# First mixer: the attention's calls placed between the k of the convolution's products

## The chip, the cores and the metric

The kernel runs on one core of one Trainium2 chip. The metric is the device time of one execution in microseconds (us). Three runs of the kernel before gave a median of 2560.59 us.

## What is computed

Two transformer blocks on 512 tokens of width 1024, all in float32. The change lies in the mixer of the first block. Cut to what matters there:

```python
px = modulate(rmsnorm(x, norm_mix), m3, m4) @ w_mix_in          # 512 tokens
pc = modulate(rmsnorm(ctx, norm_mix), mc3, mc4) @ w_mix_in      # 256 context tokens
q, k, v, gb, gc, u = split_heads(px, q_norm, k_norm)            # 8 query heads of 64, 2 key heads
qc, kc, vc, ... = split_heads(pc, q_norm, k_norm)
a  = softmax(rope(q) @ [kc, rope(k)].T / 8) @ [vc, v]           # 8 heads, 768 keys
sc = gb * short_conv3(gc * u, conv_w)                           # 512 channels
x  = x + m5 * (concat([rmsnorm(a), rmsnorm(sc)]) @ w_mix_out)
```

Products are done in three float32r passes (high times high, low times high, high times low), so that each k of a product is three matmuls per output piece.

## The kernel before

The program is traced with a framework that plans each engine's order: of the instructions that the plan takes as ready, the one that stands first in the program's text goes first. Text order is therefore a priority, and not yet the order on the engine. The semaphores come from the framework. `tc.issue_after(ins)` adds an edge of order between `ins` and the block's instructions on the same engine alone.

`run(jobs, bg)` (L180) goes through a list of jobs. A job loads its weights one job ahead, splits them (ACT makes `wh` at L159, DVE makes `wl` at L148), runs one `gemm` (L220) into one of two PSUM tiles `mm`, and evacuates the tile. After each job `bg(i)` is called. A `gemm` has a loop over k of `mm3` (L204): the three passes. After each k it counts `self.step` up and, if something is in `self.events`, calls `tick` (L211), which traces all due events inside `issue_after` of the last matmul. `later(steps, fn)` puts an event there. Other stages use it; the first mixer does not.

In `mixer1` (L623) the stages are:

- k, v and four q jobs. They use the PSUM pool `pm1`. After them `pm1` is closed and `pm2` opened in its place, with the one tile `sx` (tag `s2`, `ns2 = 1`) of the scores and two banks of tag `t`.
- The convolution: 12 jobs (`cc`, `cu`, `cb` for each of four j), each a `gemm` of 8 k over 256 and 258 columns. That is 96 k, and 24 x 2 matmuls a job.
- `r_from_acc(rc)` (L860), the norm of the convolution's output, and 8 output jobs on it (`job_out(co, f, False)`), each 4 k of 512 columns: 12 matmuls. Their evacuation (`tu`, then `x`) needs `rc`.
- `finish` (L864), which is put in as number 7 of that list, so before the eighth output job. It drains what is left of the attention and makes `ra`, the norm of the attention's output.
- 8 output jobs on the attention's output (`job_out(ao, f, True)`), whose evacuation needs `ra`.

The attention is a generator (L788). It keeps up to three units alive, of 16 in all (8 heads by two halves of the queries), and goes round them. A unit (L742) has four yields: two steps with scores (`sx` on PE, its maximum on DVE, `pp` = exp on ACT, reciprocal on DVE, scaling on ACT), one with 12 transposes and their splits (`pt`, `pth`, `ptl`), and one with 12 matmuls of probabilities by values (L776), `pv` and `at`. The fifth `next` on a unit finds its end, does no work, and the generator yields all the same (L794 to L797). So the whole attention takes 80 calls of `next(gen)`: 64 with work and 16 without. Call them n = 0 to 79. `bg` makes five of them after every job: n = 0 to 59 in the 12 jobs of the convolution, n = 60 to 79 after the first four output jobs.

The order of the calls that matter below: n = 44 and 46 are the score steps 18 and 19 (counted from 0), n = 59, 61, 62 the steps 24, 25, 26, n = 64, 65, 68, 74, 76 the steps 27 to 31, n = 63, 67, 71, 77 the transposes of units 12 to 15, n = 66, 70, 73, 78 their products by the values.

The attention's last product by the values feeds `make_y` and `sq_add` (L784, L785), these feed `ra`, and this the evacuation of the first two attention output jobs.

Of the kernel before, what the change touches and what calls it, by code (L numbers as in the profile page):

```python
# [120 lines left out]
class K:  # L121
# [501 lines left out]
    def mixer1(self, yc):  # L623
# [3 lines left out]
        with ExitStack() as es:  # L627
# [103 lines left out]
            jobs = [([(W[4], 1024)], job_k), ([(W[5], 1024)], job_v)]  # L731
# [56 lines left out]
            def attention():  # L788
                act = []
                todo = [(h, half) for h in range(8) for half in range(2)]  # L790
                while todo or act:
                    if todo and len(act) < 3:
                        act.append(unit(*todo.pop(0)))
                    for u in list(act):  # L794
                        if next(u, "end") == "end":
                            act.remove(u)
                        yield  # L797
            gen = attention()

            def bg(i):  # L800
                for _ in range(5):
                    next(gen, None)


            hold = {}
# [1 line left out]
            def job_in(nm, j):  # L807
                def go(ws):
                    t = p2.tile([P, 514], F32, name=nm, tag=nm, bufs=1) if nm != "cc" else pool.tile([P, 768], F32, name=nm, tag="to", bufs=2)
                    if nm == "cu":  # L810
                        u = pool.tile([P, 768], F32, name="cx", tag="to", bufs=2)[:, :512]
                        x_in(ws, u)
                        gcu = hold["cc"]
                        nc.vector.memset(t[:, 0:1], 0.0)
                        nc.vector.memset(t[:, 513:514], 0.0)
                        self.tt(t[:, 1:513], u, gcu[:, :512], ALU.mult)
                        w = lambda i: self.vec("conv_w", 4 * i + j)
                        self.ts(sct[j], t[:, 0:512], w(0), ALU.mult)
                        self.stt(sct[j], t[:, 1:513], w(1), sct[j], ALU.mult, ALU.add)
                        self.stt(sct[j], t[:, 2:514], w(2), sct[j], ALU.mult, ALU.add)  # L820
                    elif nm == "cc":
                        x_in(ws, t[:, :512])
                        hold["cc"] = t
                    else:
                        x_in(ws, t[:, :512])
                        self.tt(sct[j], sct[j], t[:, :512], ALU.mult)
                        self.sq_add(j, sct[j], 0, 512, p2)
                        self.dump("sc", j, sct[j])
                return go

            jobs = []
            for j in range(4):
                jobs += [([(W[10 + j], 1024)], job_in("cc", j)), ([(W[14 + j], 1024)], job_in("cu", j)),
                         ([(W[6 + j], 1024)], job_in("cb", j))]
            self.run(jobs, bg)

            g7 = pool.tile([P, 8], F32, name="g7")
            self.stt(g7, self.mx[:, 7, :], 1.0, self.vec("norm_ffn2", 0, 8), ALU.add, ALU.mult)

            def job_out(ops, f, last):  # L840
                def go(ws):
                    ps = self.mmtile()
                    self.gemm([ps[:, :512]], ws, 4, lambda k: [ops[k]])
                    t = pool.tile([P, 770], F32, name="tu", tag="tu", bufs=2)[:, :512]
                    self.tt(t, ps[:, :512], (ra if last else rc)[:, :512], ALU.mult)
                    self.stt(self.x[f], t, self.mx[:, 5, f:f + 1], self.x[f], ALU.mult, ALU.add)
                    if last:
                        self.dump("x2", f, self.x[f])
                        self.make_y(f, self.x[f], g7[:, f:f + 1], self.yh[f][:, :512], self.yl[f][:, :512])
                        for i in range(2):  # L850
                            self.split(self.yh[f][:, 512 + i:513 + i], self.yl[f][:, 512 + i:513 + i], self.mx[:, 6, f:f + 1])
                        self.sq_add(f, self.x[f], 0, 512, p2)
                return go
# [8 lines left out]
            ra = pool.tile([P, 770], F32, name="to", tag="to", bufs=2)  # L862

            def finish(ws):  # L864
                for _ in gen:
                    pass
                self.r_from_acc(ra, [(512, 0, 512)], pool, bank, n=512)

            jobs = [([(wo[f, :, 4:8, :], 512)], job_out(co, f, False)) for f in range(KD)]
            jobs.insert(7, ([], finish))  # L870
            jobs += [([(wo[f, :, 0:4, :], 512)], job_out(ao, f, True)) for f in range(KD)]
            self.run(jobs, bg)
            self.r_from_acc(self.r, [(0, 0, 256), (256, 256, 256)], pool, bank)


# [849 lines left out]
```

## Time and profile before

| | us |
|---|---|
| median of 3 runs | 2560.59 (2557.4 to 2562.12) |
| the profiled execution: time | 2563.32 |
| the profiled execution: span | 2561.5 |
| first mixer's convolution, attention and output: first to last score step begins | 679.5 to 822.1 |

The busy time of PE is a modelled one: matmuls are pipelined and their ends overlap, so gaps between starts say more than busy time. [...] Windows are in us from the span's start.

### The profile page before, as it was taken

How to read it: one execution, taken by the hardware profiler on the slowest of the kernel's cores; microseconds unless marked ns; L12 is line 12 of the kernel's file. 1: busy time of each engine (PE TensorE's matmuls, PEld its weight loads, DVE VectorE, ACT ScalarE, POOL GpSimd, SP SyncE). 2: the span in 40 equal slices, each digit the busy share in tenths (PEclk: the TensorE clock that was granted, in tenths of full speed). 3: DMA queues.
4: the chain of work that ended last, by engine and by line, in shares of the span. 5: the costliest groups of instructions: out<-in, count | busy, mean ns of one | idle time of the engine just before them, and what ended most of it. 6: DMA issues, size and time to landing. Idle time of an engine off the chain costs nothing.

```text
span 2561.5 us, 35787 instructions
## 1 busy us (share of the span) xinstructions
PE 2521.7 (98%) x13975; PEld 2171.1 (85%) x13975; DVE 1652.0 (64%) x3353; ACT 1115.9 (44%) x2052; POOL 15.6 (1%) x11
## 2 busy tenths in 40 slices
PE   7999999999999999999999999999999999999999
PEld 4889889899898888888888888888888877788887
DVE  7865664346888943335877776878888867633333
ACT  7221221234687532224677762655544444422221
POOL 2000000000000000000000000000000000000000
PEclk8999999999999999999999999999999999999999
DMA  7433543212111333333311122222222222233332
GB/s 265 143 113 107 177 145 122 66 51 81 60 38 38 100 99 99 91 103 95 101 58 58 58 84 83 73 63 80 61 74 77 75 89 88 92 94 98 96 101 84
DMA packets 85258, 235.71 MB, mean 92 GB/s; under 512 B 19840, under 2 KB 22592, under 8 KB 85088
## 3 DMA queue, kind: packets, MB, share of 16 engines
q1 hardware_dynamic: 85088, 233.42, 29.3%
q8 instruction: 110, 1.80, 0.3%
q14 instruction: 60, 0.49, 0.1%
HBM read 228.07 MB, written 5.31 MB: 91 GB/s over the span
## 4 chain that ended last, share of the span: by engine, by line
PE 91%; DVE 4%; ACT 3%; issue 1%; DMA 1%; DVEq 0%; ACTq 0%
PE mm L204 71%; PE mX L204 3%; PE mT L204 3%; PE pt L766 1%; PE pt L776 1%; PE e L1553 1%; DVE wl L148 1%; PE e L1563 1%; PE pv L1199 1%; PE sx L750 1%; PE e L1545 1%; PE e L1546 1%; PE z L204 1%; DMA araw<-wada 1%; PE e L1559 1%
## 5 line engine op out<-in xcount | busy, mean ns | idle before, releaser
L159 ACT ACTIVATE wh<-raw 128x1024 fp32r<-128x1024 f32 (+2 forms) x371 | 374.9, 1012 | 944.7 <-PE mm L204 567.1
L148 DVE TENSOR_TENSOR wl<-raw,wh 128x1024 fp32r<-128x1024 f32 (+2 forms) x371 | 431.1, 1163 | 165.6 <-ACT wh L159 160.6
L204 PE MATMUL mm<-yh,wh 128*128 128x512 f32 (+3 forms) x1552 | 455.9, 339 | 10.3 <-ACT yh L159 4.3
L204 PE MATMUL mm<-yl,wh 128*128 128x512 f32 (+3 forms) x1552 | 454.9, 338 | 0.0
L204 PE MATMUL mm<-yh,wl 128*128 128x512 f32 (+3 forms) x1552 | 451.5, 336 | 0.0
L204 PEld LDWEIGHTS mm<-yh,wh 128*128 128x128 f32 x1552 | 265.3, 189 | 44.9 <-issue 6.8
L204 PEld LDWEIGHTS mm<-yl,wh 128*128 128x128 f32 x1552 | 265.0, 189 | 29.9 <-issue 2.0
L204 PEld LDWEIGHTS mm<-yh,wl 128*128 128x128 f32 x1552 | 264.6, 189 | 29.2 <-issue 1.0
L204 PE MATMUL mm<-hl,wh 128*128 128x384 f32 (+1 forms) x704 | 227.4, 364 | 0.7 <-DVE hl L148 0.7
L204 PE MATMUL mm<-hh,wh 128*128 128x384 f32 (+1 forms) x704 | 227.3, 363 | 0.8 <-ACT hh L159 0.8
L204 PE MATMUL mm<-hh,wl 128*128 128x384 f32 (+1 forms) x704 | 227.8, 364 | 0.0
L204 PE MATMUL mm<-zh,wh 128*128 128x512 f32 x576 | 224.1, 389 | 0.0
L204 PE MATMUL mm<-zl,wh 128*128 128x512 f32 x576 | 224.1, 389 | 0.0
L204 PE MATMUL mm<-zh,wl 128*128 128x512 f32 x576 | 224.1, 389 | 0.0
L204 PEld LDWEIGHTS mm<-hh,wh 128*128 128x128 f32 x704 | 130.2, 189 | 15.0 <-ACT hh L159 1.1
L204 PEld LDWEIGHTS mm<-hl,wh 128*128 128x128 f32 x704 | 130.0, 188 | 14.8 <-DVE hl L148 1.0
L204 PEld LDWEIGHTS mm<-hh,wl 128*128 128x128 f32 x704 | 130.3, 189 | 13.8
L204 PEld LDWEIGHTS mm<-zh,wl 128*128 128x128 f32 x576 | 108.1, 188 | 22.6
L151 DVE SCALAR_TENSOR_TENSOR aacc<-araw,csil,aacc 128x1024 f32<-128x1024 f32 x70 | 88.3, 1282 | 60.4 <-DMA araw<-wada 60.3
L204 PEld LDWEIGHTS mm<-zl,wh 128*128 128x128 f32 x576 | 108.1, 188 | 22.4
L204 PEld LDWEIGHTS mm<-zh,wh 128*128 128x128 f32 x576 | 108.1, 188 | 22.3
L151 DVE SCALAR_TENSOR_TENSOR x<-mm,g,x 128x512 f32<-128x512 f32 x48 | 35.9, 747 | 115.3 <-PE mm L204 115.3
(504 smaller groups left out, 4550.0 us busy)
## 6 DMA issues: line engine op xcount, KB each, us to landing
raw<-win SPq DMA_DIRECT2D x88, 512.0 KB, 3.5
araw<-wada SPq DMA_DIRECT2D x60, 512.0 KB, 3.9
raw<-w1i SPq DMA_DIRECT2D x44, 512.0 KB, 3.7
raw<-w2i SPq DMA_DIRECT2D x44, 512.0 KB, 3.5
raw<-w3i SPq DMA_DIRECT2D x44, 512.0 KB, 3.5
raw<-wmi SPq DMA_DIRECT2D x18, 512.0 KB, 3.5
raw<-wbd SPq DMA_DIRECT2D x16, 512.0 KB, 3.7
raw<-w1o SPq DMA_DIRECT2D x16, 448.0 KB, 3.5
```

Of the source, the lines that this page charges most:

```text
L148: return self.V.tensor_tensor(out=out, in0=a, in1=b, op=op)
L151: return self.V.scalar_tensor_tensor(out=out, in0=a, scalar=s, in1=b, op0=op0, op1=op1)
L159: return self.A.activation(out=out, in_=a, func=func, bias=bias, scale=scale, **kw)
L204: last = self.T.matmul(o, lhsT=w[a], rhs=yy[b], start=start and i == 0, stop=stop and i == 2)
L750: self.T.matmul(sx[:, :512], lhsT=lq, rhs=kk[:, :512], start=i == 0, stop=i == 1)
L766: self.T.transpose(ps[:, (2 * kt + qt) * P:(2 * kt + qt + 1) * P], pr[qt][:, (2 * c + kt) * P:(2 * c + kt + 1) * P], self.cs("ident"))
L776: self.T.matmul(ps[:, :256], lhsT=vs[:, kt, g, :], rhs=pp[kt // 2][i][:, (kt % 2) * 256:(kt % 2 + 1) * 256], start=kt == 0 and i == 0, sto ...
L1199: self.T.matmul(pv[:, c0:], lhsT=a[:m, j], rhs=b, start=j == 4 and i == 0, stop=i == 2, skip_group_check=True)
L1545: self.T.matmul(ps[:, :256], lhsT=ch(kt, c), rhs=S0, start=True, stop=True)
L1546: self.T.matmul(ps[:, 256:], lhsT=ch(qt, c, 0), rhs=S0, start=True, stop=True)
L1553: self.T.matmul(ps[:, :256], lhsT=ch(XT, c, 0), rhs=vi, start=True, stop=True)
L1559: self.T.matmul(ps[:, 256:], lhsT=ch(kd, c, 0), rhs=vn, start=True, stop=True)
```

## The change

The five calls after each job are taken away. Before the convolution's jobs, 64 events are put on the step counter: call n is due after k number 3 + floor(3n/2) of what follows, counted over the `gemm`s. They are traced in `tick`, so each call's PE instructions get an edge of order behind the last matmul of that k, and in the text they stand there, ahead of the rest of the job. The 96 k of the convolution hold the calls n = 0 to 62; n = 63 is due at number 97, the first k of the first output job. Both `bg` are taken away, the one of the output jobs too. `finish` flushes the events and then drains the generator as before: n = 64 to 79 are traced there, after the text of seven output jobs.

```diff
-            def bg(i):
-                for _ in range(5):
-                    next(gen, None)
+
+            for n in range(64):
+                self.later(3 + 3 * n // 2, lambda: next(gen, None))
...
-            self.run(jobs, bg)
+            self.run(jobs)
...
             def finish(ws):
+                self.flush()
                 for _ in gen:
                     pass
                 self.r_from_acc(ra, [(512, 0, 512)], pool, bank, n=512)
...
-            self.run(jobs, bg)
+            self.run(jobs)
```

## Rows read from the trace of the kernel before

**Rows 1.** The page, parts 1 and 2.
```profile
span 2561.5 us, 35787 instructions
...
PE 2521.7 (98%) x13975; PEld 2171.1 (85%) x13975; DVE 1652.0 (64%) x3353; ACT 1115.9 (44%) x2052; POOL 15.6 (1%) x11
```

**Rows 2.** Windows of the stage; columns in the first row.
```profile
core 0: us, PE busy (x) PEld busy (x) DVE busy (x) ACT busy (x) POOL busy (x), PEclk, DMA share, GB/s
690.00:698.00 8.00, 5.48 (x35) 4.17 (x34) 6.70 (x15) 7.30 (x14) 0.00 (x0) 1.00 0.06 26
698.00:787.30 89.30, 89.18 (x691) 84.62 (x690) 73.98 (x153) 73.03 (x139) 0.00 (x0) 1.00 0.10 34
798.00:807.00 9.00, 6.94 (x30) 5.26 (x29) 8.86 (x21) 7.78 (x17) 0.00 (x0) 0.81 0.09 29
807.00:836.00 29.00, 29.00 (x173) 24.19 (x172) 24.10 (x47) 20.15 (x37) 0.00 (x0) 1.00 0.16 52
```

**Rows 3.** L750, the score steps: ns min/median/max, first and last start.
```profile
L750 PE MATMUL sx<-ksh,qs x32: 390/489/628, 679.5 to 822.1; 128*128 128x512 f32 x32
```

**Rows 4.** PE groups by form, first row 679.4 to 787.3, second 767.46 to 787.3.
```profile
L204 PE MATMUL mm<-yl,wh 128*128 128x258 f32 x76 | 21.9, 288 | 0.0
...
L204 PE MATMUL mm<-yl,wh 128*128 128x258 f32 x16 | 4.5, 282 | 0.0
```

**Rows 5.** Timeline of PE: score steps 18 and 19; columns in the first row.
```profile
start us, us, engine line op out<-in xcount [idle before <-releaser]
760.39 0.50 PE L750 MATMUL sx<-ksh,qs 128*128 128x512 f32 x1
761.19 0.28 PE L204 MATMUL mm<-yl,wh 128*128 128x256 f32 x1
767.45 0.40 PE L750 MATMUL sx<-ksh,qs 128*128 128x512 f32 x1
```

**Rows 6.** Timeline of ACT: the exp of score step 18 ends.
```profile
764.28 0.20 ACT L159 ACTIVATION_READ_ACCUMULATOR pp<-sx,st 128x1 f32 x1
```

**Rows 7.** Timeline of PE: first, last matmul of an output job, next job's first.
```profile
833.18 0.40 PE L204 MATMUL mm<-yh,wh 128*128 128x512 f32 x1
...
835.75 0.39 PE L204 MATMUL mm<-yh,wl 128*128 128x512 f32 x1
835.98 0.39 PE L204 MATMUL mm<-qs,wh 128*128 128x512 f32 x1
```

**Rows 8.** Timeline of PE: the wait for `rc`, and what follows it.
```profile
800.24 0.39 PE L204 MATMUL mm<-yh,wl 128*128 128x512 f32 x1
802.42 0.87 PE L766 MATMUL pt<-cst,pp 128*128 128x128 f32 x6 [1.80 <-ACT pp L159]
803.56 0.79 PE L204 MATMUL mm<-yh,wh 128*128 128x512 f32 x1 [0.26 <-DVE tu L148]
804.58 0.63 PE L750 MATMUL sx<-ksh,qs 128*128 128x512 f32 x1
805.86 0.63 PE L204 MATMUL mm<-yh,wl 128*128 128x512 f32 x1
```

**Rows 9.** Timeline of PE: the last two score steps.
```profile
818.72 0.50 PE L750 MATMUL sx<-ksh,qs 128*128 128x512 f32 x1
822.14 0.39 PE L750 MATMUL sx<-ksh,qs 128*128 128x512 f32 x1
```

**Rows 10.** Timeline: attention's last product, `ra` finished, third attention output job.
```profile
833.06 0.28 PE L776 MATMUL pt<-ptl,vs 128*128 128x256 f32 x1
842.06 0.69 DVE L151 SCALAR_TENSOR_TENSOR to<-rv,to 128x512 f32<-128x512 f32 x1
843.62 0.70 PE L204 MATMUL mm<-qs,wh 128*128 128x512 f32 x2 [0.82 <-DVE tu L148]
```

**Rows 11.** Windows around the wait for `rc` (columns as in Rows 2).
```profile
803.00:804.00 1.00, 0.74 (x4) 0.50 (x3) 1.00 (x2) 1.00 (x3) 0.00 (x0) 0.64 0.00 0
804.00:805.00 1.00, 1.00 (x3) 0.72 (x3) 1.00 (x4) 0.97 (x3) 0.00 (x0) 0.50 0.00 0
```

## Prediction

> **What bounds the kernel now.** I read the page first: PE is busy for 98% of the span [rows 1], so only what leaves PE without work, or lets it work slowly, can move the time much. Then I cut the first mixer into windows [rows 2]. From 698 to 787.3, the convolution with the attention between its products, PE has work for 89.18 of 89.30 us: no placing of the same work can gain there. Stalls stand at two places: 690 to 698 (5.48 busy of 8.00, 2.5 lost) and 798 to 807 (6.94 of 9.00, and a granted clock of 0.81). From 807 to 836 PE is busy for all 29.00 us again. So the most that better placing could win in this stage is those two places, some 5 to 6 us, 0.2%. What it can lose is open: it is the time that the attention takes by itself once nothing is left to lay beside it.
>
> The attention by itself is a chain. All 32 score steps share one PSUM tile, so a step starts when the exp of the step before has read it. They begin at 679.5 and the last begins at 822.1 [rows 3]: 142.6 us over 31 steps, 4.6 us each. The shortest distance that I found late in the stage is 3.42 us [rows 9], with output products in between.
>
> Where do they stand against their calls? Between 679.4 and 787.3 one of the six kinds of convolution matmul appears 76 times [rows 4], so some 20 of 96 k were done when the first score step began. By then the kernel before had made 10 calls and the new text would have made 12. The attention starts late and runs with a debt.
>
> Score step 18 begins at 760.39 and step 19 only at 767.45 [rows 5], though the exp that frees the tile ended at 764.48 [rows 6]. Sixteen of the 96 k remain at that moment [rows 4], so step 19 (n = 46) starts right after the tenth job, which is exactly where `bg` calls it. For 3 us PE had convolution products to run that stood earlier in the text, and ran them. That row is what I rest on: **a call that stands late in the text waits as long as PE has products that stand ahead of it.**
>
> **The change part by part.**
>
> Convolution, n = 0 to 62. The calls stand some five k earlier than before (n = 46 at k 72, not 80). The new edges of order bind on PE alone, behind a matmul that has long been issued, since the attention runs with a debt; so they add nothing. No semaphore is waited for anew. The calls issue no DMA, so nothing moves on SP's queue, and nothing of them is on POOL. On DVE and ACT they now stand ahead of the job's own evacuation; its cover is the second `mm` tile, which gives a job's length. Before, PE paid for such crowding 2.5 us at 690 to 698; I keep that, since calls 0 to 9 stand ahead of that evacuation in both texts. The gain is that steps 19 and on are no longer held: from 760.39 at 4.6 us a step, step 26 (n = 62) comes at 797.2, about 1.5 us earlier than now. PE has no idle time there to give back, so this gain is worth only what it takes off the end of the attention.
>
> Output jobs. Before, calls 60 to 79 stood after the first four output jobs. Now the text has seven output jobs, and only then n = 64 to 79: score steps 27 to 31, 36 transposes, four products by values. An output job is 12 matmuls from 833.18 to 835.98 [rows 7], 2.8 us. The work that stands ahead, counted from the convolution's end at 787.3: seven jobs, 19.6 us; steps 25 and 26 at 0.8 us each (760.39 to 761.19, [rows 5]), 1.6; two sets of transposes at about 1.1 (six in 0.87 with their end, [rows 8]), 2.2; a product by values, some 1.4 (an estimate from its 12 starts that end at 833.06, [rows 10]); the four matmuls for `rc`, about 1. Together 25.8 us, so PE comes free at 813.1, if it never waits for `rc`.
>
> Does it? Now the first evacuation with `rc` lets PE go on at 803.56 [rows 8]. If `rc` comes no sooner, the first two jobs and the rest are done at some 799.2, PE waits 4.4 us, step 27 slips into that hole, and the seventh job ends at 817.5. So either step 27 starts at 813.1 and four steps follow, or step 28 at 817.5 and three follow. At 3.42 us a step the last score step starts at 826.8 or 827.8, at 4.6 us at 831.5 or 831.3. The two ways agree: **826.8 to 831.5, where it now stands at 822.1**, 4.7 to 9.4 us later. I take the upper part, 8 us: 3.42 is the shortest distance that I found, and 4.6 the mean of all 31.
>
> What follows the last score step is a chain, 822.14 to 833.06 for the last product by values and 843.62 for the third attention output job, which waits for `ra` with 0.82 us of idle time [rows 9, 10]. Now the eighth output job and the first two attention jobs fill 8.4 us of it; after the change they have nothing to do with its length. Less crowding may take 1 us off, PE's pauses may add as much; both at nothing, bounds -1 and +2. The attention output jobs and all later stages are the same work and shift as a whole. Removing `bg` and adding `flush` costs nothing: all 64 events have fired when `finish` comes.
>
> The sum: the profiled execution took 2563.32 us, 2.73 above the median of the runs shown. It becomes 2571.3, and the median 2560.59 + 8 = **2568.6 us**.
>
> **The rivals.**
>
> *Not held.* If the plan finds moments when no output product is ready (a weight split late, a tile not evacuated), the steps 27 to 31 slip in, since each needs but 0.8 us of PE. Then only the gain counts: 13 steps after 760.39 at 4.6 us put the last step at 820.2, 1.9 us earlier, and with the pause before 803.56 and its slow matmuls avoided (about 2 us idle and 1.5 us slow) up to 5.4 us: 2555 to 2558.7. For it: the third and later jobs each wait for an evacuation. Against it: that evacuation is one DVE instruction of 0.7 us behind a job of 2.8 us, and [rows 5]. It decides if two or more of the five steps slip in.
>
> [...]
>
> *It does not do what it says.* The attention starts 20 k late and its pace is set by the one score tile, so "two for every three" never binds; if the plan also fills the output jobs as it does now, the order on PE hardly changes: -2 to +3 us, around 2561.
>
> **How the numbers follow.** Held as in the sum, +4 to +11 us: 0.50. Cold drain, +11 to +18: 0.12. Not held: 0.20. No effect: 0.18. The measurement can tell about 0.2%, 5.1 us, from no change. Slower by more than that: nearly all of the cold drain and 0.84 of the forecast, 0.54 together. Faster by more than that: a third of "not held", 0.07, and 0.01 for what I overlook. The same: 0.38. The range takes in "not held" at its best and all but the worst of the cold drain: 2555 to 2577.
>
> **What would show it.** Right: score steps close to 4.6 us apart up to the convolution's end; then a gap in them of 10 us or more while output jobs run without a pause; four or five score steps after the seventh output job with PE idle between them; the third attention output job near 851. Wrong: score steps among the third to seventh output jobs, or the last one before 823. [...] A new PE wait for `tg` or `tu` in the convolution would mean that crowding on DVE, which I put at nothing, is the cost.

## The result, and the profile after

The changed kernel takes 2572.41 us (median, 2572.2 to 2574.03), the kernel before 2560.28 us beside it: 12.1 us slower by the medians, which is 0.47%; the ratio on record is 1.0052 with a 95% interval of 1.0039 to 1.0066. Forecast were 2568.6 us and 2555 to 2577.

The profiled run of after, the slowest of its four, took 2574.03 us with a span of 2572.2 us. The page's part 1 looks like that of before [rows 1]:

```profile
span 2572.2 us, 35788 instructions
...
PE 2525.1 (98%) x13975; PEld 2172.9 (84%) x13975; DVE 1652.2 (64%) x3353; ACT 1119.2 (44%) x2052; POOL 15.5 (1%) x11
```

The same 13975 matmuls, and 98% again. The difference is in one stage. The first score step begins at 677.3 here and at 679.5 before [rows 3], so this run came 2.1 us earlier to the mixer (why, at the end). From that step to the end of the span it needs 2572.2 - 677.33 = 1894.87 us, before 2561.5 - 679.47 = 1882.03: **12.8 us are lost between, and all of them before 855**, since from there on the two traces run at one distance within 0.4 us. In the text below, "shifted" means 2.14 us added to a time of after, so that it can stand beside one of before.

The score steps of after, first as a group, then one by one from step 27 on, the second row being the first output product after `rc` (timeline of PE; "..." marks rows left out):

```profile
L750 PE MATMUL sx<-ksh,qs x32: 392/478/653, 677.3 to 830.8; 128*128 128x512 f32 x32
```

```profile
799.67 0.50 PE L750 MATMUL sx<-ksh,qs 128*128 128x512 f32 x1
...
804.56 0.50 PE L204 MATMUL mm<-yh,wh 128*128 128x512 f32 x1 [0.80 <-DVE tu L148]
...
818.59 0.39 PE L750 MATMUL sx<-ksh,qs 128*128 128x512 f32 x1
...
823.38 0.46 PE L750 MATMUL sx<-ksh,qs 128*128 128x512 f32 x1
...
826.88 0.51 PE L750 MATMUL sx<-ksh,qs 128*128 128x512 f32 x1
...
830.81 0.50 PE L750 MATMUL sx<-ksh,qs 128*128 128x512 f32 x1
```

Step 27 comes at 799.67, while PE waits for `rc`. Then none comes for 18.92 us, although the exp that frees the score tile for step 28 ended at 809.08 (timeline of ACT):

```profile
808.89 0.19 ACT L159 ACTIVATION_READ_ACCUMULATOR pp<-sx,st 128x1 f32 x1
```

For 9.5 us its tile was free and step 28 did not run. Windows show what PE does in that time, and what follows (columns as in Rows 2; PEclk is the granted clock of PE as a share of the full one):

```profile
698.00:787.30 89.30, 89.28 (x694) 84.92 (x693) 73.61 (x153) 73.72 (x134) 0.00 (x0) 1.00 0.11 34
...
804.50:818.50 14.00, 13.94 (x60) 11.34 (x61) 11.07 (x23) 4.36 (x7) 0.00 (x0) 1.00 0.33 97
...
834.00:854.00 20.00, 12.78 (x39) 8.94 (x40) 9.54 (x17) 7.88 (x13) 0.00 (x0) 0.66 0.04 14
```

In the gap PE runs 60 output products, five jobs of twelve, without a pause. Behind the last score step it has work for 12.78 of 20 us, and the granted clock is 0.66 in the mean. Before, the stretch around and behind the last score step was full: PE busy for 29.00 of 29 us up to 836, at 1.00 [rows 2]. What PE waits for there are the links of one chain: exp, transposes, split, product by values, evacuation, `make_y`, sum of squares (two matmuls at L275, below called the sums of `ra`), `ra`. In the timeline of PE it looks like this:

```profile
834.71 0.33 PE L766 MATMUL pt<-cst,pp 128*128 128x128 f32 x1 [1.39 <-DVE at L148]
837.44 1.54 PE L766 MATMUL pt<-cst,pp 128*128 128x128 f32 x6 [2.40 <-ACT pp L159]
839.75 1.11 PE L766 MATMUL pt<-cst,pp 128*128 128x128 f32 x4 [0.77 <-DVE ptl L148]
...
845.01 0.51 PE L204 MATMUL mm<-qs,wh 128*128 128x512 f32 x1 [1.68 <-ACT qs L159]
...
846.49 2.04 PE L275 MATMUL t<-acc,cst 128*128 128x512 f32 x2
849.90 1.22 PE L204 MATMUL mm<-qs,wh 128*128 128x512 f32 x2 [1.38 <-DVE tu L148]
...
854.34 0.63 PE L204 MATMUL mm<-qs,wh 128*128 128x512 f32 x2
```

The wait at 849.90 is not one for `ra`, which is finished on DVE only at 852.69 (last row here). It is one for the evacuation of the eighth output job, which DVE makes at 849.17, right behind the first instruction of the norm for `ra`:

```profile
848.56 0.69 DVE L156 TENSOR_SCALAR rv<-t 128x512 f32<-128x512 f32 x1 [0.88 <-PE t L275]
849.17 0.68 DVE L148 TENSOR_TENSOR tu<-mm,to 128x512 f32<-128x512 f32 x1
...
852.00 0.69 DVE L151 SCALAR_TENSOR_TENSOR to<-rv,to 128x512 f32<-128x512 f32 x1
```

The 12.8 us add up along that chain. From the first to the last score step: 153.48 us, before 142.67 [rows 3, 9], **10.81 more**. From the last score step to the end of `ra`: 852.69 - 830.81 = 21.88 us, before 842.75 - 822.14 = 20.61 [rows 9, 10], **1.27 more**. The remaining 0.8 us lie behind `ra`: the third attention output job began 0.87 us after the end of `ra` before (843.62) and begins 1.65 us after it now (854.34), since from 849.90 on a pair of output products takes 1.22 us, at a granted clock of 0.50, where it takes 0.63 at 854.34, at 1.00.

### The profile page after: what moved, and what is told of

Its sections match the earlier page's. It is cut to its first block, busy times and chain, and to the rows that moved or that the text cites. A ratio compares the mean times of both kernels' runs of the same rounds, so it can differ in the third digit from the quotient of the medians.

```text
span 2572.2 us, 35788 instructions
## 1 busy us (share of the span) xinstructions
PE 2525.1 (98%) x13975; PEld 2172.9 (84%) x13975; DVE 1652.2 (64%) x3353; ACT 1119.2 (44%) x2052; POOL 15.5 (1%) x11
## 4 chain that ended last, share of the span: by engine, by line
PE 91%; DVE 4%; ACT 3%; issue 1%; DMA 1%; SPq 0%; DVEq 0%; ACTq 0%
PE mm L204 71%; PE mX L204 3%; PE mT L204 3%; DVE wl L148 1%; PE pt L776 1%; PE pt L766 1%; PE e L1554 1%; PE sx L750 1%; PE e L1564 1%; PE pv L1200 1%; PE e L1546 1%; PE e L1547 1%; PE z L204 1%; PE e L1560 1%; DMA araw<-wada 0%
```

## The experiments

One measure is used for all kernels. In windows of 2 us from 670 to 880, "without work" is the sum of 2 minus PE's busy time, and "slow" the sum of PE's busy time times (1 minus granted clock): an estimate of what the same work would have saved at the full clock, from pairs like the one above (1.22 us at 0.50, 0.63 at 1.00). The ratio of each kernel is to runs of the kernel before on the same chip (their median is 2560.3 us for after and e1 to e4, 2561.0 for the others).

| kernel | median us | ratio to before, 95% | without work | slow | both |
|---|---|---|---|---|---|
| before | 2560.3 | | 7.1 | 1.6 | 8.6 |
| after | 2572.4 | 1.0039 to 1.0066 | 12.4 | 6.6 | 19.0 |
| e1, five per output job | 2558.85 | 0.9986 to 1.0004 | 6.0 | 0.0 | 6.0 |
| e2, removed only | 2580.47 | 1.0067 to 1.0095 | 17.2 | 8.5 | 25.7 |
| e3, eighty placed | 2561.01 | 0.9996 to 1.0014 | 7.6 | 0.0 | 7.6 |
| e4, third | 2572.83 | 1.0038 to 1.0063 | 13.1 | 5.1 | 18.2 |
| e5, third, own scratch | 2561.86 | 0.9996 to 1.0014 | 8.3 | 0.0 | 8.3 |
| e6, first, own scratch | 2558.48 | 0.9981 to 0.9998 | 5.7 | 0.0 | 5.7 |
| e7, filler | 2571.83 | 1.0028 to 1.0053 | 5.1 | 0.0 | 5.1 |
| e8, first, shared | 2578.22 | 1.0051 to 1.0079 | 16.4 | 4.7 | 21.0 |
| e9, changed, own scratch | 2574.23 | 1.0038 to 1.0066 | 14.4 | 6.5 | 21.0 |
| e10, before, own scratch | 2560.47 | 0.9987 to 1.0005 | 6.4 | 3.3 | 9.7 |

Sums may be off by 0.1 from rounding. Apart from e7, which has 50 matmuls more, the kernels fall into two groups in the last column as they do in the first: up to 9.7 us in those near 2560, 18 and more in those above 2572. The measure isn't exact and does not order the kernels within a group: after has 10.4 more than before and lost 12.8, e8 has 12.4 more and lost 17.3 by the medians. What makes up the rest is open. Of the 6.6 of after, 1.5 lie at 690 to 698, at the start of the convolution, and have nothing to do with its end.

**e1: the calls given back to the output jobs** (the last `run` is that of the output jobs).

```diff
+            def bg(i):
+                for _ in range(5):
+                    next(gen, None)
             for n in range(64):
                 self.later(3 + 3 * n // 2, lambda: next(gen, None))
...
-            self.run(jobs)
+            self.run(jobs, bg)
```

> The changed kernel with one part of the change undone: the 64 calls stay one by one in the convolution, but each output job is again followed by five calls, so that the last 16 are spread behind the first four output jobs. Theory (the 16 calls that now stand behind seven output jobs are the whole cost): the gap in the score steps goes, the last one is back near 820 to 823 in the time axis of the kernel before, and the median is 2556 to 2562. Rival (the one-by-one calls in the convolution, with their edges of order, cost something by themselves): the time stays above 2566.

Measured: 2558.85 us, the same as before within its interval. The score steps 27 to 29 (timeline of PE):

```profile
801.14 0.50 PE L750 MATMUL sx<-ksh,qs 128*128 128x512 f32 x1
...
805.97 0.50 PE L750 MATMUL sx<-ksh,qs 128*128 128x512 f32 x1 [0.75 <-ACT pp L159]
...
810.22 0.48 PE L750 MATMUL sx<-ksh,qs 128*128 128x512 f32 x1
```

The last comes at 819.43. The gap is gone, with the 64 calls still one by one in the convolution. That placing, its edges and the crowding on DVE and ACT cost nothing that could be measured in the time.

**e2: the kernel before, only the calls behind the output jobs removed.** The convolution's jobs keep their `bg`; the line is that of the output jobs.

```diff
-            self.run(jobs, bg)
+            self.run(jobs)
```

> The kernel before with only the other part of the change: after each convolution job five calls as before, none any more after the output jobs, so that the last 20 calls stand behind seven output jobs. Theory: this alone shows the loss, 2570 to 2577, a little above the changed kernel since four more calls (score step 26 among them) are left for the end. Rival (placing in the convolution costs): 2560 to 2565.

Measured: 2580.47 us, 20 us more than before, and 3.5 more than the upper end of what I expected. So this part of the change alone brings the whole loss and more. It leaves four calls more for the end than the changed kernel, which is 8 us faster. The trace shows by what: step 25, the first score step of the calls left for the end, slips in at 796.75 while PE has only the wait for `rc` ahead of it. Then nothing of the attention runs in that hole, PE stands still for 4.0 us (its longest wait for `tu`), and steps 26 to 31 all stand behind the output jobs, the last at 837.37. In the changed kernel step 27 and a product by values still run in the hole.

**e3: all eighty calls placed.**

```diff
-            for n in range(64):
+            for n in range(80):
```

> The changed kernel with 80 calls placed one by one at the same pace, instead of 64, so that the last 16 are placed among the k of the first six or so output jobs (four k each). Theory: no score step stands behind a block of output jobs any more; the gap goes and the time is 2556 to 2563. Rival (the order edges or the crowding of DVE and ACT cost): above 2566.

Measured: 2561.01 us, the same as before. The loss comes from the 16 calls that the number 64 leaves out, not from placing one by one.

**e4: the rest of the attention behind three output jobs instead of seven.**

```diff
-            jobs.insert(7, ([], finish))
+            jobs.insert(3, ([], finish))
```

> The changed kernel with the rest of the attention put behind three output jobs instead of seven. The computation is the same. Theory (a late call waits for all output products ahead of it in the text, and what stands behind it fills its pauses): the gap in the score steps shrinks by four jobs of 2.8 us, and the five jobs behind it fill the pauses of PE and keep its clock up, so the time falls by about 8 to 12 us from the changed kernel: 2559 to 2565. Rival (the end of the attention costs the same wherever it stands, since its chain has to be run without the convolution's products anyhow): 2570 or more.

Measured: 2572.83 us, no gain at all. My theory failed here, and this run taught most. The last score step comes at 821.84, as early as before [rows 9], and yet the time is that of after. So **the last score step doesn't set the time by itself.** What PE did at the end of the attention (timeline, then the group of output products from 836 to 851):

```profile
836.90 1.61 PE L275 MATMUL t<-acc,cst 128*128 128x512 f32 x2 [3.15 <-DVE acc L148]
839.89 0.80 PE L204 MATMUL mm<-yh,wh 128*128 128x512 f32 x1 [1.38 <-DVE tu L148]
```

```profile
L204 PE MATMUL mm<-yh,wh x12: 388/396/796, 839.9 to 849.6; 128*128 128x512 f32 x12
```

PE stood still 3.15 us for `acc`, though output products stood behind in the text: one kind of three appears 12 times after the sums of `ra`, so 36 products, three whole jobs, ran only then. DVE tells what held them:

```profile
838.55 0.69 DVE L156 TENSOR_SCALAR rv<-t 128x512 f32<-128x512 f32 x1 [1.80 <-PE t L275]
839.15 0.68 DVE L148 TENSOR_TENSOR tu<-mm,to 128x512 f32<-128x512 f32 x1
...
840.66 0.69 DVE L148 TENSOR_TENSOR tu<-mm,to 128x512 f32<-128x512 f32 x1
```

The evacuations of the fourth and fifth job come right behind the first instruction of the norm for `ra`, 18 us after the last of their products (821.0). Both the evacuation of an output job and the scratch of `r_from_acc` take a tile `tu`, two buffers in rotation, and in the text `ra` takes its one ahead of those jobs. Two jobs sat in the two PSUM tiles, and the third found none. The next three runs test that.

**e5 and e6: an own scratch tile for `ra`, the rest of the attention behind three jobs, and ahead of all.** The diff is that of e5; e6 has 0 in place of 3.

```diff
-    def r_from_acc(self, r, spans, pool, bank, n=D):
+    def r_from_acc(self, r, spans, pool, bank, n=D, a=None):
...
-        a = pool.tile([P, 770], F32, name="ra", tag="tu", bufs=2)
+        a = a if a is not None else pool.tile([P, 770], F32, name="ra", tag="tu", bufs=2)
...
-                self.r_from_acc(ra, [(512, 0, 512)], pool, bank, n=512)
+                self.r_from_acc(ra, [(512, 0, 512)], pool, bank, n=512, a=sct[3])
...
-            jobs.insert(7, ([], finish))
+            jobs.insert(3, ([], finish))
```

> The kernel with the rest of the attention behind three output jobs, and one edit more: the scratch tile of the sum for ra no longer comes out of the two rotating buffers named tu, from which each output job takes its own tile too, but is a tile that is dead by then. Theory (behind the rest of the attention only two output jobs could run, since the buffer of the third is the scratch of ra, which is read last of all; so the pauses of the end stood without products): the 36 output products that ran after the sums of ra now run between the last transposes and products by values, PE has no pause over 1 us and no window at the low clock before ra, and the median is 2556 to 2563. Rival (what the end of the attention waits for, by itself, sets the time, and products in its pauses change nothing): 2568 or more.

> As the run with the own scratch tile, with the rest of the attention ahead of all output jobs instead of behind three. Theory (what stands first in the text goes first, and output jobs behind it fill its pauses as long as buffers let them): score steps at 4 to 5 us right after the wait for rc, the last at 818 to 822, and 2555 to 2562, no worse than the kernel before. Rival (with all output jobs behind it, they would be used up late and pile up after the attention's end, as 36 products did with three jobs ahead): 2565 or more.

Measured: e5 2561.86 us, 11 us under e4 by the scratch tile alone. e6 2558.48 us, the only one of the ten whose interval lies below 1, by 0.1%; its last score step comes at 817.83, where 818 to 822 was expected. In e5 DVE evacuates output jobs in the middle of the end (826.98 and 831.10), PE has work from 804 to 836 without a pause, and the sums of `ra` wait for nothing on PE (timelines):

```profile
826.98 0.68 DVE L148 TENSOR_TENSOR tu<-mm,to 128x512 f32<-128x512 f32 x1
...
831.10 0.69 DVE L148 TENSOR_TENSOR tu<-mm,to 128x512 f32<-128x512 f32 x1 [0.86 <-PE mm L204]
```

```profile
833.25 1.05 PE L275 MATMUL t<-acc,cst 128*128 128x512 f32 x2
```

No pause over 1 us was expected before `ra`; one of 2.3 us was found, behind the sums of `ra`, where PE waits for `ra` itself. In e6 PE is busy for 40.00 of 40 us from 816 to 856.

**e8: as e6, with the shared scratch.**

> The rest of the attention ahead of all eight output jobs, with the scratch of ra left in the two rotating buffers: the run with the same place and an own scratch, less that one edit. Theory (behind the rest of the attention only two output jobs can run before ra is done, whatever stands there): 72 of the 96 convolution output products start after the sums of ra, in one block; pauses of over 10 us in all and windows at the low clock before; 2574 to 2581, slower than with three jobs ahead. Rival (the shared buffers are not what held the jobs, and the gain of the own scratch came from where that edit put the instructions): within 4 us of the run with the own scratch, 2555 to 2562.

Measured: 2578.22 us against 2558.48 of e6, which differs from it by the scratch tile alone. The last score step comes at 815.39, **earlier than in any other kernel, and the time is the second longest.** The group of output products behind the sums of `ra`, and the window in which PE had nothing else:

```profile
L204 PE MATMUL mm<-yh,wh x24: 388/395/793, 834.1 to 851.7; 128*128 128x512 f32 x24
```

```profile
818.00:838.00 20.00, 11.30 (x35) 8.16 (x36) 9.92 (x17) 7.24 (x12) 0.00 (x0) 0.66 0.00 0
```

72 products, six jobs, ran after the sums of `ra` instead of in the pauses ahead of them. That the shared scratch holds the jobs is thus shown twice (e4 against e5, e8 against e6). By which rule of the plan they do is read from the order on DVE and was not tested.

**e9 and e10: the own scratch in the changed kernel, and in the kernel before.** The edit of `r_from_acc` of e5, and nothing else.

> The changed kernel, seven output jobs ahead of the rest of the attention, with the one edit of the own scratch. Theory (only the eighth output job stands behind, and it ran in the pauses already; the attention's output jobs need ra themselves, and have two PSUM tiles between them): nothing left to fill the pauses with, so no gain: 2569 to 2574. Rival (the shared scratch is the cause of the loss in the changed kernel too): 2558 to 2564.

> The kernel before with the one edit of the own scratch. Theory (five calls behind each of the first four output jobs leave the rest of the attention only the last steps, so the shared buffer held little): within 2 us of the kernel before, 2557 to 2562, so that what the run with everything behind the attention gains comes from its place and not from this edit. Rival (the wait of 0.82 us before the third attention output job and the pause at rc go with it): 2554 to 2557.

Measured: e9 2574.23 us, as slow as after, and 0.2 above what I expected. e10 2560.47 us, as fast as before. So the scratch isn't the cause in the changed kernel: with seven jobs ahead one job is left behind, and the attention's output jobs need `ra` themselves. That the gain of e6 comes from its place is likely and not shown: the intervals of e6 and e10 overlap.

**e7: matmuls that nobody needs, in the pauses.** The changed kernel, and behind the convolution's output jobs, ahead of the attention's, one job more:

```diff
+            def fill(ws):
+                ps = self.mmtile()
+                for i in range(50):
+                    self.T.matmul(ps[:, :512], lhsT=co[i % 4][0][:, :P], rhs=co[i % 4][0], start=i == 0, stop=i == 49)
...
+            jobs.append(([], fill))
```

> The changed kernel with 50 matmuls of 512 columns more, as a job of its own between the convolution's and the attention's output jobs; their sum is read by nobody, and they only give TensorE work while the rest of the attention runs. They take the place of the some ten attention output products that ran there, which now come 2.2 us of work later. Theory (part of the loss is the low clock in the pauses): no window before ra at the low clock; the last transposes, the last product by values, the matmuls of ra and the first output products after it take half of what they took, 4 to 5 us together, so that the time is 2 to 3 us under the changed kernel, 2568 to 2572, and the way from the last score step to the end of ra shrinks from 21.9 to 20 or less. Rival (the pauses themselves are the loss, the clock is no more than a sign): that way stays near 21.9 and the time rises by the 2.2 us to some 2574 to 2577.

Measured: 2571.83 us with 50 matmuls more, 0.6 below after. The window, then six of the last transposes and the end of `ra`:

```profile
834.00:854.00 20.00, 19.86 (x93) 15.23 (x92) 11.60 (x20) 9.54 (x16) 0.00 (x0) 1.00 0.04 14
```

```profile
837.31 0.88 PE L766 MATMUL pt<-cst,pp 128*128 128x128 f32 x6
...
850.19 0.68 DVE L151 SCALAR_TENSOR_TENSOR to<-rv,to 128x512 f32<-128x512 f32 x1
```

With work in the pauses the clock stays at 1.00, and six transposes take 0.88 us where they took 1.54 at 0.50. From the last score step to the end of `ra` it is 850.87 - 831.76 = 19.1 us, not 21.9; counted from step 28 (818.45 here), since the last step moved by itself, 32.4 against 34.1. So **the low clock lengthens the chain by some 1.7 us**, as far as the matmuls added do not delay it themselves. Of the time it costs between 0.6 us, the difference of the medians, and 2.5 us, the difference of the two traces: from step 28 to the third attention output job it is 33.22 us here (to 851.67) and 35.75 in after. Twelve products of the attention's output, one job, ran ahead of the sums of `ra` in after and behind them here (I had counted ten). They cost little here: `ra` ends at 850.87, and the third attention output job begins at 851.67.

## Why the prediction was right, point by point

**What bounds the kernel: right.** From 698 to 787.3 PE had work for 89.28 of 89.30 us after the change as before; nothing was to be won there, and nothing was lost. The loss is outside of it.

**A late call waits for the products ahead of it: right, but not by the row it rested on.** The gap of 18.92 us full of output products shows it, with step 28 held for 9.5 us after its tile was free; e1 and e3 take the gap away, e2 brings it alone. [rows 5] I read wrongly: I said that in the 3 us between the end of the exp and step 19 PE ran convolution products. It ran four transposes, the twelve matmuls of a product by values and only eight convolution matmuls, some 1 us of the 3. The last matmul of that product, then four of the eight, then step 19:

```profile
766.87 0.28 PE L776 MATMUL pt<-ptl,vs 128*128 128x256 f32 x1
766.98 0.40 PE L204 MATMUL mm<-yl,wh 128*128 128x256 f32 x2
767.22 0.40 PE L204 MATMUL mm<-yh,wl 128*128 128x256 f32 x2
767.45 0.40 PE L750 MATMUL sx<-ksh,qs 128*128 128x512 f32 x1
```

In after the call stands eight k earlier in the text. Here the end of the exp on ACT, then step 19 on PE behind the same product:

```profile
764.01 0.20 ACT L159 ACTIVATION_READ_ACCUMULATOR pp<-sx,st 128x1 f32 x1
...
764.45 0.28 PE L776 MATMUL pt<-ptl,vs 128*128 128x256 f32 x1
764.56 0.39 PE L750 MATMUL sx<-ksh,qs 128*128 128x512 f32 x1
```

The exp ends at 764.21 and step 19 follows 0.35 us later, yet from step 18 to step 19 it is 6.71 us, where 7.06 were before. So most of that distance was the attention's own work, and the place of the call was worth some 0.35 us. I had looked at when the tile came free and at where the call stood, and not at what ran in between. That the rule drawn from this row held at the output jobs was, as far as the row goes, luck.

**The convolution at no cost: right.** e1 and e3 bound it, 0.9986 to 1.0014 between them, for the time as a whole; for `rc` see below. The gain on the attention was forecast at 1.5 us by step 26; it came at 795.65, shifted 797.8, where 798.63 was before: 0.8 us.

**The sum, +8, measured +12.1: three terms.** (1) The hole at `rc`: as forecast, step 27 slipped into it. But I took over the moment at which `rc` let PE go on, 803.56 [rows 8]. It was 804.56, shifted 806.70, **3.1 us later, and that is the term that was mis-sized.** DVE finishes the two halves of `rc` and starts the first evacuation, in before:

```profile
802.02 0.75 DVE L151 SCALAR_TENSOR_TENSOR to<-rv,to 128x256 f32<-128x256 f32 x2
...
802.81 1.29 DVE L148 TENSOR_TENSOR tu<-mm,to 128x512 f32<-128x512 f32 x2
```

and in after:

```profile
799.24 0.42 DVE L151 SCALAR_TENSOR_TENSOR to<-rv,to 128x256 f32<-128x256 f32 x1
...
801.09 0.95 DVE L753 TENSOR_REDUCE st<-sx 128x1 f32<-128x768 f32 x1
...
802.88 0.42 DVE L151 SCALAR_TENSOR_TENSOR to<-rv,to 128x256 f32<-128x256 f32 x1
...
803.82 1.28 DVE L148 TENSOR_TENSOR tu<-mm,to 128x512 f32<-128x512 f32 x2
```

The halves came one behind the other, 3.6 us apart, with the maximum of step 27 and splits of the attention between them. I had costed what the earlier calls put on DVE at nothing, since a second `mm` tile covers the convolution's evacuations; `rc` has no such cover, and the attention that came 0.8 us sooner stood ahead of it. The traces of the experiments show that this comes with the placing: counted from the first score step, the second half of `rc` starts at 125.3 to 125.6 us in all nine kernels that place the calls one by one, and at 122.9 to 123.0 in the three that make five after a job (before, e2, e10). e1, e3, e5 and e6 have the late `rc` too and are no slower than before, so a late `rc` need not cost anything where other work fills PE. Which of the instructions ahead of it on DVE is to blame no run isolates. Five jobs then took 804.56 to 818.6, the 2.8 us each of the forecast, so the seventh ended at 820.7 (shifted), not 817.5. (2) Three score steps followed in 12.22 us, 4.07 each, between the 3.42 and 4.6 that bounded them. With (1) the last step stands 10.8 us later, where 4.7 to 9.4 were forecast. (3) The chain behind it, put at nothing within -1 and +2, took 1.27 more, and 0.8 came behind `ra`. The third attention output job, forecast near 851, began at 856.5 (shifted). The +12.1 is above the +4 to +11 of the forecast itself and inside the +11 to +18 of *cold drain*, the rival with a low clock in the pauses of the end; the stated range took it in because it covered both, which is in part luck.

**"The eighth job and two attention jobs have nothing to do with the length": right for the chain, wrong as a way to count.** The chain is 21.9 us in after and 22.0 in e8 (815.39 to the end of `ra` at 837.44), 20.6 in before. But the time is not the last score step plus a constant, as my sum had it: e8 has its last step 15 us before that of after, counted from the first step (138.05 against 153.48), and is 5 to 6 us slower. What counts is how much of PE's work is left to stand beside the chain. In after the eighth job and nine products of the attention's output ran between the last four score steps, where PE was busy for 11.60 of 12.22 us, so the pauses that I had named as a sign between these steps did not come there; they came behind the last one, where three products were left ahead of the sums of `ra`. Only because nearly nothing was left did the two ways of counting agree.

**The rivals.** *Not held* fell with the gap. *It does not do what it says* holds for the convolution half (e1), and falls for the other (e2). *Cold drain*, to which I gave 0.12, came in part: the granted clock was 0.50 from 838 to 842 and 0.58 from 850 to 854. Its +11 to +18 is the +4 to +11 of the forecast and 7 us for the low clock, which no run shows; e7 gives 0.6 to 2.5. Of my 7, 2.5 were for five score steps, an estimate from one before that took 1.28 us (804.58 to 805.86) at 0.50 [rows 8, 11], against 0.8 [rows 5]. Here the five ran at a granted clock of 1.00: step 27 at 799.67, the last four in 818.59 to 830.81, and the clock fell behind them. The result, +12.1, is therefore a forecast with a late `rc` plus a fraction of that rival, and not either alone.

## What to carry to other kernels

Before calls of a background task are moved to the front, count how many remain for the end, and which work of the busiest engine is still unspent there: a chain that runs alone costs its own pauses, wherever its last step stands. Put the rest of such a task ahead of the work that is to fill its pauses (e6, no slower than before), and check that nothing in its text takes a rotating buffer that the filling work needs too (e4 and e8 against e5 and e6). When a stall is blamed on an order, read every instruction that ran on the engine since the wait could have ended, in both the cases that are compared.

## What was unexpected in the hardware

Two pauses of under 1 us stood ahead of a fall of the clock, which moved the time of a whole run. In the first FFN, whose text the change doesn't touch, PE pauses twice within 2 us. Before:

```profile
381.72 0.75 PE L204 MATMUL mm<-hh,wh 128*128 128x384 f32 x2 [0.77 <-ACT hh L159]
383.19 1.02 PE L204 MATMUL mm<-hl,wh 128*128 128x384 f32 x2 [0.71 <-DVE hl L148]
```

```profile
380.00:388.00 8.00, 6.52 (x26) 5.67 (x25) 6.18 (x10) 1.89 (x3) 0.00 (x0) 0.79 0.48 147
```

After:

```profile
381.00 0.75 PE L204 MATMUL mm<-hh,wh 128*128 128x384 f32 x2 [0.32 <-ACT hh L159]
382.46 0.78 PE L204 MATMUL mm<-hl,wh 128*128 128x384 f32 x2 [0.71 <-DVE hl L148]
```

```profile
380.00:388.00 8.00, 6.96 (x37) 6.12 (x37) 5.55 (x9) 1.90 (x3) 0.00 (x0) 1.00 0.50 151
```

One pause is 0.45 us longer, and the clock is 0.79 in the mean where it is 1.00: 8.00 x 0.21, by estimate some 1.7 us. With the 0.45 us itself that is the 2.1 us by which the profiled run of after came earlier to the mixer, a bit under half of what runs of one kernel differ by here (2557.4 to 2562.12 for before). The other traces agree: in before, e1 and e4 the first pause was 0.77 to 1.05 us, the clock went to 0.50 behind it, and the mixer's first score step came at 679.0 to 679.5. In the other nine it was at most 0.45 us, the clock stayed at 1.00 there, and that step came at 675.4 to 677.6. So this is a matter of the run and not of the change.
